# An encoder layer on one core: another order for the first weight chunks, and the modulated input with priority and in full precision on ScalarE

## The chip, the core and the metric

The kernel runs on one core of a Trainium2 chip. A core has TensorE (PE: matmuls, with weight loads shown apart as PEld), VectorE (DVE), ScalarE (ACT), GpSimd (POOL), and SyncE (SP), whose queue issues most transfers. Each engine works through its own queue in order; semaphores join them. The metric is device time in microseconds (us): the median of the runs.

## The reference

One layer of an encoder: 256 tokens of width 2048, all in float32. The part that matters here is the start: six modulation vectors from the condition c, the modulated input, and the projection to q, k and v.

```python
c_act = jax.nn.silu(c)
mod = c_act @ mod_w[i] + mod_b[i]
sh_m, sc_m, g_m, sh_f, sc_f, g_f = jnp.split(mod, 6, axis=-1)
hmix = x * (1.0 + sc_m[:, None, :]) + sh_m[:, None, :]
proj = h @ w_qkv + b_qkv        # h is hmix, (256, 2048) @ (2048, 3072)
...
x = layer_norm(DEEPNORM_ALPHA * x + (1.0 + g_m[:, None, :]) * y, ...)
hff = x * (1.0 + sc_f[:, None, :]) + sh_f[:, None, :]
u = jnp.square(jax.nn.relu(hff @ w1 + b1))
```

Behind the projection come windowed attention with rotary positions and sinks, the output projection, a layer norm, and an MLP of 8192 hidden units with a second layer norm.

## The kernel before

**Precision.** A matmul of two float32 operands is made of three matmuls in a rounded format. Each operand is split into a high part (the value rounded) and a low part (the value less its high part). The three products are high by high, high by low and low by high; low by low is left out. `mm3` (line 497) issues the three for one output of 128x512 and one 128-row tile of the inner dimension. Its three lines are 498, 499 and 500. The output gathers in a PSUM bank, a `pa` tile. There are five such banks.

**Weights.** All large weights come in chunks of 128x2048 float32 (1,024 KB) through one list, planned ahead of time. `Stream.loads` issues their transfers on SP's queue, in the order of the list, whenever one of eight buffers is free. ScalarE copies each half of a chunk to its high part (`wh`, line 247), and VectorE subtracts to get the low part (`wl`, line 218). There are five buffers for each. `Stream.pump` does this ahead of the matmuls.

**Modulation.** The list also holds chunks of the modulation weights. Such a chunk is used up at once by `Mod.step`: either PE multiplies it by c into the bank `pm` (line 307), or VectorE accumulates it into a tile (lines 343 and 345). The last chunk of a group closes the sum: four matmuls add VectorE's part, and ScalarE copies the result to `mrow` (line 361).

**Groups.** The inner dimension of 2048 has 16 tiles of 128. They are cut into six groups of 1, 1, 2, 4, 4 and 4 tiles, so that the projection can start before the whole modulation is known. Groups 0 and 1 share the first three weight chunks (`FIRST`); groups 2 to 5 have chunks of their own, 3 or 6 each. When group g's modulation is complete, `modulated(g)` makes the group's input: `columns` transposes `mrow` on PE (lines 370 and 377) and adds the bias on VectorE (371, 373 and 383, 384). Then for each tile ScalarE makes the high part of x * scale + shift (line 519), VectorE makes the same in full precision (line 520), and VectorE subtracts to get the low part (line 521).

**Projection.** `qkv_first` works on the first three chunks and `qkv` on the others. For each chunk and each of the two halves of 128 tokens a bank gathers 3 matmuls per tile. `evict` then empties the banks: the first time by a copy on ScalarE (line 535), later by an addition on VectorE (line 537). Some chunks (`CARRY`) leave their banks open for the next.

**What sets the order.** The transfers follow the list, written at lines 425 to 449. Within an engine the order is set by a scheduler when the program is built: it takes the instructions in the order of the code, moves them by its own estimates of time, and may let one overtake another. `tc.keep_in_program_order` pins an instruction; `Stream.pinned` does so while `S.pin` is set, that is, up to line 624. The code from line 604 to 633 runs the groups one after another: `S.vecs(n)` uses up n modulation chunks, `run(qkv(g, c), mid)` runs a weight chunk and calls `mid` after its first half.

Of the kernel before, what the change touches and what calls it, by code (L numbers as in the profile page):

```python
# [2 lines left out]

# [1 line left out]

# [6 lines left out]
F32 = mybir.dt.float32  # L12
F32R = mybir.dt.float32r
I32 = mybir.dt.int32
AF = mybir.ActivationFunctionType
OP = mybir.AluOpType
# [4 lines left out]
S = 256  # L21
NT = S // 128
# [26 lines left out]
def hybrid_kernel(ctx: ExitStack, tc: tile.TileContext, a, out: bass.AP):  # L49
    nc = tc.nc  # L50
    cst = ctx.enter_context(tc.tile_pool(name="cst", bufs=1))
    sml = ctx.enter_context(tc.tile_pool(name="sml", bufs=4))
# [21 lines left out]
    def g4(dt=F32):  # L74
        return gen.tile([128, 1024], dt, tag="g4", name="g4")

    def f32(x):
        return x.bitcast(F32)
# [5 lines left out]
    modmb, modfb, lnT = (pack[:, 80 + 32 * n:112 + 32 * n].rearrange("p (n k) -> p n k", n=2) for n in range(3))  # L84
# [340 lines left out]
    wq = lambda g, c: S.plan(a["wqkv"][m_mix[g][1] * 6 // 4 + c])  # L425
    m_mix[0][0].plan(2)
    S.plan(a["wqkv"][0])
    m_mix[1][0].plan(2)
    S.plan(a["wqkv"][1])
    S.plan(a["wqkv"][2])  # L430

    S.side[len(S.q)] = lambda: load_x(1)
    m_mix[2][0].plan(3)
    wq(2, 1)
    m_mix[2][0].plan(1)
    for g in range(2, G):
        n = len(ORDER[g])
        if g + 1 < G:
# [58 lines left out]
    def mm3(ps, xh, xl, wh, wl, start, stop):  # L497
        nc.tensor.matmul(ps, xh, wh, start=start, stop=False)  # L498
        nc.tensor.matmul(ps, xh, wl, start=False, stop=False)  # L499
        S.prev = nc.tensor.matmul(ps, xl, wh, start=False, stop=stop).ins  # L500
# [3 lines left out]
    def load_x(n):  # L504

        k0, nk = XK[n]
        xt = g4()
        (nc.sync if n else nc.scalar).dma_start(xt[:, :nk * 256], a["xT"][:, k0 * 256:(k0 + nk) * 256])
        for k in range(nk):
            xts[k0 + k] = xt[:, k * 256:k * 256 + 256]  # L510

    def modulated(g):
        m, k0, nk = m_mix[g]
        columns(m, modmb, (scm, shm), k0, nk)
        hh, hl = g4(F32R), g4(F32R)
        for k in range(nk):
            s = slice(k * 256, k * 256 + 256)
            xt, sc, sh = xts.pop(k0 + k), scm[:, k0 + k:k0 + k + 1], shm[:, k0 + k:k0 + k + 1]
            tc.keep_in_program_order(nc.scalar.activation(hh[:, s], xt, AF.Identity, scale=sc, bias=sh))  # L519
            tc.keep_in_program_order(nc.vector.tensor_scalar(xt, xt, sc, sh, op0=OP.mult, op1=OP.add))  # L520
            tc.keep_in_program_order(nc.vector.tensor_sub(hl[:, s], xt, f32(hh[:, s])))  # L521
        held[g] = hh, hl

    half = {}
# [17 lines left out]
    def qkv_first(n):  # L542

        wh, wl = S.main()
        for i, (g, p) in enumerate(FIRST[n]):
            hh, hl = held[g]
            c = CORD[p]
            opens = c not in half
            held_back = ((g, n), p) in CARRY or (n == 1 and g == 0)
            pss = half.pop(c, None) or banks()  # L550
            for t in range(NT):
                s = slice(t * 128, t * 128 + 128)
                mm3(pss[t], hh[:, s], hl[:, s], wh(i), wl(i), opens, c in acc and not held_back)
            if i % 2:
                S.done()
            if held_back:
                half[c] = pss
            else:
                evict(c, pss)
            if i == 1:  # L560
                yield

    def qkv(g, ch):

        _, k0, nk = m_mix[g]
        hh, hl = held[g]
        wh, wl = S.main()
        per = 4 // nk
        for ci in range(per):
            p = ch * per + ci  # L570
            c = CORD[p]
            go_on, held_back = c in half, ((g, ch), p) in CARRY
            pss = half.pop(c, None) or banks()
            for k2 in range(0, nk, 2):
                for t in range(NT):
                    for k in (k2, k2 + 1):
                        s = slice(k * 256 + t * 128, k * 256 + t * 128 + 128)
                        mm3(pss[t], hh[:, s], hl[:, s], wh(ci * nk + k), wl(ci * nk + k),
                            k == 0 and not go_on, k == nk - 1 and not held_back)
                S.done()  # L580
                if per == 1 and k2 == 0:
                    yield
            if held_back:
                half[c] = pss
            else:
                evict(c, pss)
            if per == 2 and ci == 0:
                yield

    def run(gen, mid=()):  # L590
        next(gen)
        for f in mid:
            f()
        for _ in gen:
            pass
# [16 lines left out]
    idle(6)  # L612
    msk = masks()
    S.nh, S.nl = 5, 4
    S.pace = 1
    run(qkv_first(0))
    S.vecs(2)
    run(qkv_first(1), [lambda: modulated(1)])
    trig = rotary_tables()
    run(qkv_first(2))  # L620
    S.vecs(4)
    modulated(2)
    S.pace = VECS
    S.pin = False
    for x, (g, c) in enumerate(qk_order):
# [208 lines left out]
    for n in range(21):  # L834
# [35 lines left out]
        if n == 12:  # L870
            g1 = gate(m_gm)
        if n == 16:
            warm = sml.tile([128, 1], F32, name="warm")
            nc.scalar.activation(warm, eps, AF.Sqrt)
            st = [sml.tile([128, 4, 6], F32, name=f"st{t}", bufs=2) for t in range(NT)]


# [298 lines left out]
```

## Time and profile before

| | before |
|---|---|
| median of 3 runs | 1095.94 us (1095.34 to 1098.32) |
| the profiled execution | 1100.0 us, its span 1098.2 us |
| PE idle from 0 to 75.45 us | 10.85 us |
| PE idle from 75.45 to 140 us | 2.23 us |
| PE idle from 140 to 231 us | 0.22 us |
| PE idle from 231 us to the end | 17.27 us |
| mean granted clock of PE | 0.991 |

The idle times are the length of a stretch less PE's busy time in it. In a row of the timeline the columns are start, duration (both in us), engine, line, operation, the tile written, the tiles read, shapes, and the count; in brackets stands the idle time in front and what ended it. Matmul ends are modelled and overlap: a matmul of 128x512 is shown with 0.39 us, but the next starts 0.23 us later. "x16" for a modulation step on PE is one chunk.

### The profile page before, as it was taken

How to read it: one execution, taken by the hardware profiler on the slowest of the kernel's cores; microseconds unless marked ns; L12 is line 12 of the kernel's file. 1: busy time of each engine (PE TensorE's matmuls, PEld its weight loads, DVE VectorE, ACT ScalarE, POOL GpSimd, SP SyncE). 2: the span in 40 equal slices, each digit the busy share in tenths (PEclk: the TensorE clock that was granted, in tenths of full speed). 3: DMA queues.
4: the chain of work that ended last, by engine and by line, in shares of the span. 5: the costliest groups of instructions: out<-in, count | busy, mean ns of one | idle time of the engine just before them, and what ended most of it. 6: DMA issues, size and time to landing. Idle time of an engine off the chain costs nothing.

```text
span 1098.2 us, 15487 instructions
## 1 busy us (share of the span) xinstructions
PE 1067.6 (97%) x6098; PEld 863.1 (79%) x6098; DVE 804.2 (73%) x1162; ACT 522.0 (48%) x806; POOL 30.0 (3%) x54
## 2 busy tenths in 40 slices
PE   8889999998999999999999999999999999999995
PEld 6657677665677799988888888888888888888884
DVE  4597899978899877754588889756666557665676
ACT  5333346765673537643344543344453334544340
POOL 1000000001000000000000010001000000000001
PEclk9989999999999999999999999999999999999998
DMA  9999987789985996555578788866555555557511
GB/s 384 425 427 425 427 357 280 271 297 379 377 315 201 361 360 244 185 192 192 195 301 303 272 313 306 312 220 225 184 189 190 197 196 186 178 185 267 191 75 77
DMA packets 43337, 292.70 MB, mean 267 GB/s; under 512 B 5104, under 2 KB 5232, under 8 KB 9472
## 3 DMA queue, kind: packets, MB, share of 16 engines
q1 hardware_dynamic: 39312, 279.85, 66.9%
q0 software_dynamic: 3200, 10.50, 2.7%
q10 hardware_dynamic: 752, 1.35, 0.3%
q8 instruction: 48, 0.79, 0.3%
q14 instruction: 25, 0.20, 0.0%
HBM read 289.57 MB, written 2.11 MB: 266 GB/s over the span
## 4 chain that ended last, share of the span: by engine, by line
PE 86%; DVE 7%; DMA 4%; ACT 2%; issue 1%; DVEq 0%; ACTq 0%
PE pa L995 16%; PE pa L500 15%; PE pa L498 15%; PE pa L499 15%; PE pa L996 8%; PE pa L972 3%; PE pa L971 3%; PE pa L973 3%; PE pm L307 3%; DVE wl L218 2%; DMA raw<-in_modm 2%; DMA raw<-in_modf 1%; DVE g L345 1%; DMA raw<-in_wqkv 1%; PE pa L687 1%; PE pa L743 1%
## 5 line engine op out<-in xcount | busy, mean ns | idle before, releaser
L218 DVE TENSOR_TENSOR wl<-raw,wh 128x1024 fp32r<-128x1024 f32 x332 | 403.9, 1223 | 223.6 <-ACT wh L247 222.9
L247 ACT CAST wh<-raw 128x1024 fp32r<-128x1024 f32 x332 | 347.1, 1051 | 441.3 <-PE pa L500 228.6
L498 PE MATMUL pa<-wh,g 128*128 128x512 f32 x816 | 324.1, 398 | 5.1 <-ACT g L519 2.6
L500 PE MATMUL pa<-wh,g 128*128 128x512 f32 x816 | 318.9, 392 | 4.1 <-DVE g L521 3.0
L499 PE MATMUL pa<-wl,g 128*128 128x512 f32 x816 | 320.0, 392 | 0.0
L995 PE MATMUL pa<-g,wh 128*128 128x512 f32 x768 | 270.1, 397 | 0.0
L996 PE MATMUL pa<-g,wl 128*128 128x256 f32 x768 | 214.9, 280 | 0.0
L498 PEld LDWEIGHTS pa<-wh,g 128*128 128x128 f32 x816 | 153.9, 189 | 46.8 <-issue 7.5
L500 PEld LDWEIGHTS pa<-wh,g 128*128 128x128 f32 x816 | 153.5, 188 | 41.2 <-DVE g L521 6.0
L499 PEld LDWEIGHTS pa<-wl,g 128*128 128x128 f32 x816 | 153.9, 189 | 33.0 <-issue 2.4
L995 PEld LDWEIGHTS pa<-g,wh 128*128 128x128 f32 x768 | 144.2, 188 | 36.0 <-issue 0.8
L996 PEld LDWEIGHTS pa<-g,wl 128*128 128x128 f32 x768 | 144.8, 189 | 0.1
L345 DVE SCALAR_TENSOR_TENSOR g<-raw,cact,g 128x1024 f32<-128x1024 f32 x65 | 82.6, 1280 | 2.8 <-DMA raw<-in_modf 2.3
L972 PE MATMUL pa<-g,wh 128*128 128x256 f32 x256 | 72.7, 285 | 0.4 <-DVE g L915 0.4
L971 PE MATMUL pa<-g,wh 128*128 128x256 f32 x256 | 72.5, 286 | 0.0
L973 PE MATMUL pa<-g,wl 128*128 128x256 f32 x256 | 72.3, 283 | 0.0
L307 PE MATMUL pm<-raw,cact 128*32 128x256 f32 (+2 forms) x776 | 48.8, 375 | 5.9 <-DMA raw<-in_modf 3.2
L971 PEld LDWEIGHTS pa<-g,wh 128*128 128x128 f32 x256 | 48.8, 192 | 1.3 <-issue 0.8
L972 PEld LDWEIGHTS pa<-g,wh 128*128 128x128 f32 x256 | 49.1, 192 | 0.9 <-DVE g L915 0.8
L973 PEld LDWEIGHTS pa<-g,wl 128*128 128x128 f32 x256 | 49.1, 192 | 0.0
L345 DVE SCALAR_TENSOR_TENSOR g4b<-raw,cact,g4b 128x1024 f32<-128x1024 f32 x32 | 40.7, 1280 | 9.0 <-DMA raw<-in_modgf 8.8
L307 PEld LDWEIGHTS pm<-raw,cact 128*32 128x32 f32 x776 | 20.9, 112 | 25.9 <-issue 11.5
(165 smaller groups left out, 741.6 us busy)
## 6 DMA issues: line engine op xcount, KB each, us to landing
raw<-in_w SPq DMA_DIRECT2D x64, 1024.0 KB, 4.9
raw<-in_w1b SPq DMA_DIRECT2D x48, 1024.0 KB, 5.0
raw<-in_modm SPq DMA_DIRECT2D x32, 1024.0 KB, 14.8
raw<-in_modf SPq DMA_DIRECT2D x32, 1024.0 KB, 6.9
raw<-in_wqkv SPq DMA_DIRECT2D x24, 1024.0 KB, 12.8
raw<-in_modgm SPq DMA_DIRECT2D x16, 1024.0 KB, 7.5
raw<-in_wo SPq DMA_DIRECT2D x16, 1024.0 KB, 7.5
raw<-in_w1a SPq DMA_DIRECT2D x16, 1024.0 KB, 7.6
```

What stands on the lines that cost most here:

```text
L218: self.pinned(nc.vector.tensor_sub(l, r, f32(self.hs[n])))
L247: self.pinned(nc.scalar.copy(h, s))
L307: i = nc.tensor.matmul(self.ps[32 * j:32 * j + 32, :w], lhsT[j] if type(lhsT) is list else lhsT, rhs[j], start=self.first, stop=stop)
L345: nc.vector.scalar_tensor_tensor(p[:, :e], s, cact[:, kt:kt + 1], p[:, :e], op0=OP.mult, op1=OP.add)
L498: nc.tensor.matmul(ps, xh, wh, start=start, stop=False)
L499: nc.tensor.matmul(ps, xh, wl, start=False, stop=False)
L500: S.prev = nc.tensor.matmul(ps, xl, wh, start=False, stop=stop).ins
L971: nc.tensor.matmul(o, wh(w, 128), hh, start=new, stop=False)
L972: nc.tensor.matmul(o, wh(w, 128), hl, start=False, stop=False)
L973: nc.tensor.matmul(o, wl(w, 128), hh, start=False, stop=end)
L995: nc.tensor.matmul(ps, wh(k, 128), hb, start=k == 0, stop=False)
L996: nc.tensor.matmul(ps[:, :256], wl(k, 128), hb[:, :256], start=False, stop=k == NK - 1)
```

## The change

Six edits, all in the start of the kernel up to the end of the projection.

1. In the list of transfers the second weight chunk moves ahead of group 1's two modulation chunks, and all four of group 2's modulation chunks stand together ahead of group 2's first weight chunk.
2. The work on the first three weight chunks is cut into its twelve parts (`qkv_first` yields after each), and the modulation chunks and `modulated(1)`, `modulated(2)`, `rotary_tables()` are placed between them by hand.
3. `modulated` is put under `tc.high_priority()` for groups 3 to 5; the pinned instructions in it remain pinned for groups 0 to 2 alone.
4. In `modulated`, the full-precision x * scale + shift is made by ScalarE for all groups but the first.
5. In `qkv`, the two matmuls with the input's high part come first for both halves of the tokens and both tiles; the matmuls with the input's low part follow.
6. An activation that should load a table early (`warm`) is left out. In the program before, the scheduler had placed it at the very start of ScalarE's queue.

```diff
     m_mix[0][0].plan(2)
     S.plan(a["wqkv"][0])
+    S.plan(a["wqkv"][1])
     m_mix[1][0].plan(2)
-    S.plan(a["wqkv"][1])
     S.plan(a["wqkv"][2])
-
     S.side[len(S.q)] = lambda: load_x(1)
-    m_mix[2][0].plan(3)
+    m_mix[2][0].plan(4)
+
     wq(2, 1)
-    m_mix[2][0].plan(1)
...
     def modulated(g):
         m, k0, nk = m_mix[g]
-        columns(m, modmb, (scm, shm), k0, nk)
-        hh, hl = g4(F32R), g4(F32R)
-        for k in range(nk):
-            s = slice(k * 256, k * 256 + 256)
-            xt, sc, sh = xts.pop(k0 + k), scm[:, k0 + k:k0 + k + 1], shm[:, k0 + k:k0 + k + 1]
-            tc.keep_in_program_order(nc.scalar.activation(hh[:, s], xt, AF.Identity, scale=sc, bias=sh))
-            tc.keep_in_program_order(nc.vector.tensor_scalar(xt, xt, sc, sh, op0=OP.mult, op1=OP.add))
-            tc.keep_in_program_order(nc.vector.tensor_sub(hl[:, s], xt, f32(hh[:, s])))
+
+        with nullcontext() if S.pin else tc.high_priority():
+            columns(m, modmb, (scm, shm), k0, nk)
+            hh, hl = g4(F32R), g4(F32R)
+            for k in range(nk):
+                s = slice(k * 256, k * 256 + 256)
+                xt, sc, sh = xts.pop(k0 + k), scm[:, k0 + k:k0 + k + 1], shm[:, k0 + k:k0 + k + 1]
+                S.pinned(nc.scalar.activation(hh[:, s], xt, AF.Identity, scale=sc, bias=sh))
+                if g:
+                    S.pinned(nc.scalar.activation(xt, xt, AF.Identity, scale=sc, bias=sh))
+                else:
+                    S.pinned(nc.vector.tensor_scalar(xt, xt, sc, sh, op0=OP.mult, op1=OP.add))
+                S.pinned(nc.vector.tensor_sub(hl[:, s], xt, f32(hh[:, s])))
         held[g] = hh, hl
...
-            if i % 2:
-                S.done()
             if held_back:
                 half[c] = pss
             else:
                 evict(c, pss)
-            if i == 1:
-                yield
+            if i % 2:
+                S.done()
+            yield
...
             for k2 in range(0, nk, 2):
-                for t in range(NT):
-                    for k in (k2, k2 + 1):
-                        s = slice(k * 256 + t * 128, k * 256 + t * 128 + 128)
-                        mm3(pss[t], hh[:, s], hl[:, s], wh(ci * nk + k), wl(ci * nk + k),
-                            k == 0 and not go_on, k == nk - 1 and not held_back)
+
+                for x in range(2):
+                    for t in range(NT):
+                        for k in (k2, k2 + 1):
+                            s = slice(k * 256 + t * 128, k * 256 + t * 128 + 128)
+                            w = ci * nk + k
+                            if x == 0:
+                                nc.tensor.matmul(pss[t], hh[:, s], wh(w), start=k == 0 and not go_on, stop=False)
+                                nc.tensor.matmul(pss[t], hh[:, s], wl(w), start=False, stop=False)
+                            else:
+                                S.prev = nc.tensor.matmul(pss[t], hl[:, s], wh(w), start=False,
+                                                          stop=k == nk - 1 and not held_back).ins
                 S.done()
...
-    S.pace = 1
-    run(qkv_first(0))
+
+    S.pace = 0
+    steps = (x for n in range(3) for x in qkv_first(n))
+
+    def parts(n):
+        for _ in range(n):
+            next(steps, None)
+
+    parts(2)
+    S.vecs(1)
+    parts(1)
+    S.vecs(1)
+    modulated(1)
+    parts(4)
+    S.vecs(1)
+    trig = rotary_tables()
+    parts(1)
+    S.vecs(1)
+    parts(2)
     S.vecs(2)
-    run(qkv_first(1), [lambda: modulated(1)])
-    trig = rotary_tables()
-    run(qkv_first(2))
-    S.vecs(4)
     modulated(2)
+    parts(3)
     S.pace = VECS
...
         if n == 16:
-            warm = sml.tile([128, 1], F32, name="warm")
-            nc.scalar.activation(warm, eps, AF.Sqrt)
             st = [sml.tile([128, 4, 6], F32, name=f"st{t}", bufs=2) for t in range(NT)]
```

What the built programs make of it shows at three places. Lines of the changed kernel have other numbers: 520 and 522 are the two activations and 525 the subtraction in `modulated`, 541 the eviction on VectorE, 585, 586 and 588 the three matmuls in `qkv`.

The first place is VectorE around the second of group 4's weight chunks. `wl_1086` and `wl_1156` are that chunk's low parts, `g4_1031` is the accumulator of group 5's modulation, `pa_1070` and `pa_1071` are the banks of group 4's first weight chunk, and `g4_1108`, `g4_1109` are group 4's input, high and low. Before:

```order
L343 TENSOR_SCALAR g4_1031<-raw_864,cact_110 128x1024
L345 SCALAR_TENSOR_TENSOR g4_1031<-raw_864,cact_110,g4_1031 128x1024
L345 SCALAR_TENSOR_TENSOR g4_1031<-raw_906,cact_110,g4_1031 128x1024 x2
L218 TENSOR_TENSOR wl_1086<-raw_942,wh_1062 128x1024
L218 TENSOR_TENSOR wl_1156<-raw_942,wh_1084 128x1024
L345 SCALAR_TENSOR_TENSOR g4_1031<-raw_960,cact_110,g4_1031 128x1024
L520 TENSOR_SCALAR g4_602<-g4_602,scm_112,shm_113 128x256
L345 SCALAR_TENSOR_TENSOR g4_1031<-raw_960,cact_110,g4_1031 128x1024
L521 TENSOR_TENSOR g4_1109<-g4_602,g4_1108 128x256
```

The same place in VectorE's queue in the changed program:

```order
L345 SCALAR_TENSOR_TENSOR g4_1031<-raw_864,cact_110,g4_1031 128x1024
L525 TENSOR_TENSOR g4_1109<-g4_614,g4_1108 128x256 x4
L345 SCALAR_TENSOR_TENSOR g4_1031<-raw_906,cact_110,g4_1031 128x1024
L541 TENSOR_TENSOR g4_276<-g4_276,pa_1070 128x512
L345 SCALAR_TENSOR_TENSOR g4_1031<-raw_906,cact_110,g4_1031 128x1024
L541 TENSOR_TENSOR g4_276<-g4_276,pa_1071 128x512
L218 TENSOR_TENSOR wl_1086<-raw_942,wh_1062 128x1024
L218 TENSOR_TENSOR wl_1156<-raw_942,wh_1084 128x1024
```

The input's low part has moved ahead of the accumulations, and both evictions of the first chunk's banks now stand ahead of the second chunk's low parts. At the borders between the second and third and the third and fourth of group 3's chunks both evictions likewise stand ahead of the next low part, without an accumulation between them.

The second place is ScalarE around the end of group 5's modulation. `wh_1062`, `wh_1084` are the high parts of group 4's second weight chunk, `wh_1154`, `wh_1172` those of its third and last, `mrow_1150` is group 5's modulation and `g4_1258` the high part of group 5's input. Before:

```order
L247 CAST wh_1084<-raw_942 128x1024
L519 ACTIVATE g4_1108<-g4_602,shm_113,scm_112 128x256 x4
L361 COPY mrow_1150<-pm_1020 128x256
L247 CAST wh_1154<-raw_1056 128x1024
L247 CAST wh_1172<-raw_1056 128x1024
L247 CAST wh_1188<-raw_1060 128x1024
L247 CAST wh_1210<-raw_1060 128x1024
L247 CAST wh_1226<-raw_1066 128x1024
L247 CAST wh_1248<-raw_1066 128x1024
L519 ACTIVATE g4_1258<-g4_844,shm_113,scm_112 128x256 x4
```

The same place in ScalarE's queue in the changed program:

```order
L247 CAST wh_1084<-raw_942 128x1024
L361 COPY mrow_1150<-pm_1020 128x256
L520 ACTIVATE g4_1258<-g4_844,shm_113,scm_112 128x256 x2
L522 ACTIVATE g4_844<-g4_844,shm_113,scm_112 128x256 x2
L520 ACTIVATE g4_1258<-g4_844,shm_113,scm_112 128x256 x2
L522 ACTIVATE g4_844<-g4_844,shm_113,scm_112 128x256 x2
L247 CAST wh_1154<-raw_1056 128x1024
L247 CAST wh_1172<-raw_1056 128x1024
```

Eight activations of group 5's input now stand between the copy of its modulation and the first cast of group 4's last weight chunk; before, six casts stood there and the four activations came behind them.

The third place is PE at the same end of group 5's modulation. `pm_1020` is its bank, `pt_1252` its transposes, `pa_1196` and `pa_1197` are the banks of group 4's second chunk, `pa_1234` and `pa_1235` those of its last. Before:

```order
L500 MATMUL pa_1196<-wh_1062,g4_1109 128x512
L307 MATMUL pm_1020<-raw_1034,cact_110 32x256 x8
L307 MATMUL pm_1020<-g4_1031,onesf_95 32x256 x4
L500 MATMUL pa_1197<-wh_1062,g4_1109 128x512
L498 MATMUL pa_1197<-wh_1062,g4_1108 128x512
L499 MATMUL pa_1197<-wl_1086,g4_1108 128x512
L500 MATMUL pa_1197<-wh_1062,g4_1109 128x512
L498 MATMUL pa_1196<-wh_1084,g4_1108 128x512
```

The same place in PE's queue in the changed program:

```order
L588 MATMUL pa_1196<-wh_1084,g4_1109 128x512 x2
L588 MATMUL pa_1197<-wh_1084,g4_1109 128x512 x2
L307 MATMUL pm_1020<-raw_1034,cact_110 32x256 x8
L307 MATMUL pm_1020<-g4_1031,onesf_95 32x256 x4
L377 MATMUL pt_1252<-ident_89,mrow_1150 128x128 x2
L585 MATMUL pa_1234<-wh_1154,g4_1108 128x512
L585 MATMUL pa_1235<-wh_1154,g4_1108 128x512
L586 MATMUL pa_1234<-wl_1174,g4_1108 128x512
```

Before, 16 matmuls of group 4's second chunk and two of its last stood between the closing matmuls of the modulation and the transposes; now the transposes follow at once, and the last chunk's matmuls come behind them.

More of the change, by code (lines that the diff above doesn't have):

```diff
@@ L1 @@
 import math
-from contextlib import ExitStack
+from contextlib import ExitStack, nullcontext
 import numpy as np
```

## Prediction

> **What bounds the kernel now.** I read the page first, then the waits of PE, then busy time by stretches, then the timeline of each engine from 38 to 150 us.
>
> ```profile
> span 1098.2 us, 15487 instructions
> ...
> PE 1067.6 (97%) x6098; PEld 863.1 (79%) x6098; DVE 804.2 (73%) x1162; ACT 522.0 (48%) x806; POOL 30.0 (3%) x54
> ```
>
> TensorE (PE) is busy 97% of the span, so time is lost only where PE idles or runs slowly. The stretches say where:
>
> ```profile
> 47.00:75.45 28.45, 24.83 (x155) 16.20 (x154) 27.84 (x38) 7.09 (x10) 1.91 (x2) 0.99 1.01 426
> 75.45:140.00 64.55, 62.32 (x348) 45.33 (x349) 52.14 (x68) 22.70 (x29) 0.00 (x0) 0.95 1.01 427
> 140.00:231.00 91.00, 90.78 (x466) 63.70 (x464) 89.20 (x165) 60.56 (x138) 1.23 (x2) 1.00 0.76 297
> ```
>
> The columns are length, busy PE, PEld, DVE, ACT and POOL, granted clock, DMA share, GB/s. Up to 140 us the DMA engines are full, so a chunk of 1,024 KB arrives every 2.5 us (1.049 MB by 427 GB/s) in either order. From 140 us PE is without a gap and transfers have slack. A shift of PE at 140 us therefore reaches the end of the kernel, unless a later wait absorbs it. The two largest waits that the change can reach are these:
>
> ```profile
> PE pa L500 <- DVE g L521: 3.0, 3, 2.2
> PE pa L498 <- ACT g L519: 2.6, 2, 2.4
> ```
>
> Both are waits for the modulated input: its rounded part from ScalarE (L519) and the rest from VectorE (L521).
>
> **The change part by part.** I call weight chunk c of group g (g,c); group 4 runs (4,1), (4,2), (4,0). I compare the instant at which PE starts (4,0), the last chunk before PE stays full.
>
> Part 1, the early order and the table loads, I cost at nothing. On SP's queue one weight transfer passes the two of group 1's modulation, and the fourth of group 2's passes (2,1); nothing else moves there, and POOL's queue stays as it was. Before, the start and the second and third chunk of group 3's modulation look like this:
>
> ```profile
> 11.32 0.27 ACT L361 COPY mrow<-pm 128x128 f32<-128x128 f32 x1 [3.28 <-PE pm L307]
> ...
> 44.33 0.75 DVE L343 TENSOR_SCALAR g<-raw,cact 128x1024 f32<-128x1024 f32 x1 [4.04 <-DMA raw<-in_modm]
> 48.95 1.07 PE L307 MATMUL pm<-raw,cact 128*32 128x256 f32 x16
> ```
>
> The 44.33 is a landing, so the third chunk lands at 44.33 + 2.5 = 46.8. With its second weight chunk sooner, PE ends the first three weight chunks at about 41, not just before 48.95: the last chunk of group 2's modulation lands 5.5 chunks ahead of 46.8, at 33.2, and behind it stand at most 24 matmuls (5.5) and two modulation steps (2.2). But in the new order both of group 3's PE chunks stand ahead of nearly all of group 2's matmuls, so PE waits until 46.8, and VectorE, in order, until 44.33. The gain ends in a wait for DMA. That wait of 6 us also covers what group 1's modulation loses, one transfer or 2.5 us; without it, that would show. The two table loads and the warm-up leave ScalarE's start, where it idles 3.28 us for PE anyway.
>
> Part 2, group 3 starts sooner. Before:
>
> ```profile
> 71.25 0.17 DVE L384 TENSOR_SCALAR scm<-scm 128x4 f32<-128x4 f32 x1
> ...
> 72.90 1.99 ACT L247 CAST wh<-raw 128x1024 fp32r<-128x1024 f32 x2 [5.19 <-DMA raw<-in_wqkv]
> 74.80 2.07 ACT L519 ACTIVATE g<-g,shm,scm 128x256 fp32r<-128x256 f32 x4
> ...
> 75.45 0.79 PE L498 MATMUL pa<-wh,g 128*128 128x512 f32 x1 [2.39 <-ACT g L519]
> 76.17 1.94 PE L307 MATMUL pm<-raw,cact 128*32 128x256 f32 x16
> ...
> 90.67 1.07 PE L307 MATMUL pm<-raw,cact 128*32 128x256 f32 x16
> ```
>
> The scale was ready at 71.42, but L519 stood behind two casts that waited for a landing. Now it stands ahead. VectorE's queue from 44.33 to the scale holds 7 accumulations at 1.2, 8 low parts at 1.15, 10 evictions at 0.6 and 1.1 of others: 25.1 us, hence 69.4; PE's own work, with a stretch at half clock after its wait, gives 70.4. With 0.6 for L520, PE starts at 71.05 instead of 75.45: **-4.4**. The half clock goes too: the same step took 1.94 at 76.17 and 1.07 at 90.67, and the clock columns
>
> ```profile
> 70.00:80.00 10.00, 7.61 (x47) 3.97 (x46) 9.25 (x18) 3.97 (x6) 0.95 (x1) 0.75 1.02 429
> 80.00:90.00 10.00, 10.00 (x42) 8.19 (x41) 7.99 (x9) 4.10 (x4) 0.00 (x0) 0.91 1.01 428
> ```
>
> lost 2.5 + 0.9 = 3.4 us of clock, some of it before PE started; I take **-2.9**. The wait for L521 goes as well, since its full-precision operand now comes from ScalarE:
>
> ```profile
> 123.31 0.50 PE L500 MATMUL pa<-wh,g 128*128 128x512 f32 x1 [2.23 <-DVE g L521]
> ...
> 134.26 0.62 PE L498 MATMUL pa<-wh,g 128*128 128x512 f32 x2
> ...
> 142.32 0.50 PE L500 MATMUL pa<-wh,g 128*128 128x512 f32 x1 [0.21 <-DVE g L521]
> ```
>
> That is **-2.2**, and -0.2 at 142.32. Row 134.26 is the start of (4,0) before. From 75.45 that is 58.8 us, of which 58.8 - 2.9 - 2.2 = 53.7 is work that stays.
>
> Part 3, new waits at chunk borders. Prices, from VectorE's and PE's timeline:
>
> ```profile
> 96.71 1.28 DVE L345 SCALAR_TENSOR_TENSOR g<-raw,cact,g 128x1024 f32<-128x1024 f32 x1
> 97.90 0.68 DVE L537 TENSOR_TENSOR g<-g,pa 128x512 f32<-128x512 f32 x1
> 98.50 2.35 DVE L218 TENSOR_TENSOR wl<-raw,wh 128x1024 fp32r<-128x1024 f32 x2
> ...
> 92.00 0.40 PE L499 MATMUL pa<-wl,g 128*128 128x512 f32 x1
> 92.24 0.40 PE L500 MATMUL pa<-wh,g 128*128 128x512 f32 x1
> ```
>
> By the distances of starts an accumulation holds VectorE 1.19, an eviction 0.60, a low part 1.2; a matmul step is 0.23 and ends 0.16 behind its step. The new order does all products with the high part first, so a chunk's two banks close in its last four matmuls, and VectorE has the two evictions ahead of the next chunk's low part. PE has only 4 x 0.23 = 0.92 to cover it: two matmuls of the other bank and two that need no low part. At two borders of group 3 the wait is 0.16 + 0.60 + 0.60 + 1.2 - 0.92 = 1.65; at a third one eviction stands ahead: 1.05. At (4,1) to (4,2) an accumulation stands between the evictions: 0.16 + 0.60 + 1.19 + 0.60 + 1.2 - 0.92 = 2.85. At the end of group 5's modulation eviction, accumulation, eviction, accumulation stand ahead of PE's closing matmuls, with two matmuls and one modulation chunk as cover: 0.16 + 0.60 + 1.19 + 0.60 + 1.28 - 0.46 - 1.09 = 2.3. Together **+9.5**: the closing matmuls end at 71.05 + 53.7 + 9.5 = 134.25.
>
> Part 4, (4,0) behind group 5's modulation. Before and after it is a question of what ScalarE does next:
>
> ```profile
> 130.63 0.37 ACT L361 COPY mrow<-pm 128x256 f32<-128x256 f32 x1 [13.38 <-PE pm L307]
> 130.90 4.84 ACT L247 CAST wh<-raw 128x1024 fp32r<-128x1024 f32 x5
> ...
> 134.72 0.39 PE L377 MATMUL pt<-ident,mrow 128*128 128x128 f32 x2
> ```
>
> Before, the casts of (4,0) followed the copy at once, and PE still had 16 matmuls of (4,2). Now PE has ended (4,2), and eight activations with priority stand ahead of the cast: copy 0.4, transposes 0.45, scale 0.45, eight activations 8 x 0.52 = 4.15 (four took 2.07 above), cast 1.05: **+6.5** from 134.25 to 140.75. The full-precision activation has no row. Its ends are 0.41, VectorE's operation that it replaces, and 0.60, a whole L519 without overlap:
>
> ```profile
> 50.91 0.41 DVE L520 TENSOR_SCALAR g<-g,scm,shm 128x256 f32<-128x256 f32 x1
> ...
> 37.49 0.60 ACT L519 ACTIVATE g<-g,shm,scm 128x256 fp32r<-128x256 f32 x1
> ```
>
> L519 on the same engine and shape is nearest, so 0.52; the ends give 0.4 us less or more. Behind the first two matmuls the low part is missing for 1.2 - 0.46 = 0.75, while the transposes (0.35) no longer come there: **+0.4**. After an idle 6 us a half clock is likely, as it came after 2.39 us above. Its shorter form stands here:
>
> ```profile
> 30.00:40.00 10.00, 8.73 (x84) 6.34 (x85) 3.18 (x7) 2.85 (x4) 0.00 (x0) 0.83 1.01 424
> ```
>
> 0.17 of 10 us is **+1.7**. Bounds: nothing, and three such (behind the 2.85, the 2.3 and the 6), 5.1.
>
> The Trainium skill ("TensorE: Matmul & The Clock Gate", section on HAM oscillation) asks for idle gaps over about 3.4 us before the clock halves; the gap of 2.39 us in front of 75.45 had already brought it, so the trace does not agree with that bound. By the page only the 6 us gap pays and the sum stands; by the trace the 2.85 gap may pay too, 1.7 more.
>
> Sum: (4,0) starts at 140.75 instead of 134.26, +6.5; with 0.4, 1.7 and -0.2, **+8.4 us**. The profiled execution took 1100.0 (its span 1098.2), so 1108.4 there; it lies 4.1 above the median of 1095.94, so I put the median at **1104**. VectorE's relief of 15 operations at 0.41 (6.2 us) I cost at nothing: from 75 us it waits for PE's banks.
>
> **The rivals.** (a) Faster. The intended reading: low parts are ready at the borders, because VectorE reaches the evictions before PE needs the next chunk. Then -4.4 - 2.9 - 2.4 remain, but (4,0) itself caps it:
>
> ```profile
> L202 SPq DMA_DIRECT2D raw<-in_wqkv x1: 328/328/328, 117.9 to 117.9; - x1
> ...
> DMA to landing us min/median/max: 7.5/7.5/7.5
> ```
>
> It lands at 125.4, castable at 126.5, so at most 134.3 - 126.5 = 7.8 us: 1088. Against it: the evictions stand ahead in the queue, and ScalarE cannot cast before the activations. It decides at the (4,1) border: less than 0.5 us of wait there means this rival. (b) The change does not do what it says: the delay is absorbed. VectorE is busy 89.2 of 91 us from 140 to 231; its 6.2 us less could come back there: 8.4 - 6.2, 1098. Against it: those operations lie before 140. (c) Slower still. Six later chunks have the same matmul order with VectorE full; if each eviction is 4 x 0.23 late, 5.5 us more: 1110.
>
> **How the numbers follow.** Forecast 0.64, (a) 0.14, (b) 0.12, (c) 0.10. Forecast: 8.4 with the clock between 0 and 5.1 instead of 1.7 and the activations 0.4 either way gives 6.3 to 12.2, and my 71.05 may be off by 1.5: 1100.7 to 1109.6. The range takes in (b) and half of (c): 1094 to 1110, leaving out about 0.19. A measurement here can tell 0.3%, 3.3 us, from no change. Faster by more: (a) 0.14; within: most of (b), 0.11; slower: 0.75.
>
> **What would show it.** In the new trace: PE idle from about 41 to 47; group 3 from about 71 at full clock; no wait for L521's successor; waits of PE for low parts (L218) of 1 to 3 us between 80 and 125; one of about 6 us for a cast near 134 to 141. If PE starts (4,0) before 134, I am wrong in sign, and the border waits are where.

## The result, and the profile after

| | before | after |
|---|---|---|
| median | 1096.62 us of 4 runs (1095.34 to 1098.32) | 1109.82 us of 4 runs (1107.93 to 1111.45) |
| ratio after / before | | 1.0119, 95% interval 1.0096 to 1.0142 |
| the profiled execution | 1100.0, span 1098.2 | 1111.45, span 1109.6 |

The change makes the kernel slower: by 13.2 us in the medians, by 11.45 between the two profiled executions. The forecast was 8.4 between profiled executions and 1104 us for the median.

First the waits of PE in the changed kernel (what it waited for: us in all, times, the longest):

```profile
span 1109.6 us, 15476 instructions
...
PE pa L586 <- DVE wl L218: 7.0, 4, 2.8
PE pa L585 <- ACT wh L247: 5.5, 1, 5.5
PE pm L307 <- DMA raw<-in_modm: 4.9, 2, 3.8
...
PE pm L307 <- DVE g L345: 2.3, 1, 2.3
```

The waits for the modulated input (2.6 and 3.0 us before) are gone. In their place stand four waits for low parts at the borders between chunks, one for a cast, and one for an accumulation, ahead of the closing matmuls of group 5's modulation (the closing wait): 14.8 us together. The timeline of PE shows the three largest, and VectorE's shows what stood ahead of the low part:

```profile
122.01 0.61 PE L585 MATMUL pa<-wh,g 128*128 128x512 f32 x2
125.42 0.50 PE L586 MATMUL pa<-wl,g 128*128 128x512 f32 x1 [2.80 <-DVE wl L218]
125.76 0.48 PE L585 MATMUL pa<-wh,g 128*128 128x512 f32 x1
...
136.85 0.64 PE L307 MATMUL pm<-g,onesf 128*32 128x256 f32 x8 [2.31 <-DVE g L345]
137.99 0.44 PE L377 MATMUL pt<-ident,mrow 128*128 128x128 f32 x2 [0.49 <-ACT mrow L361]
143.91 1.22 PE L585 MATMUL pa<-wh,g 128*128 128x512 f32 x2 [5.49 <-ACT wh L247]
```

```profile
121.75 0.69 DVE L541 TENSOR_TENSOR g<-g,pa 128x512 f32<-128x512 f32 x1 [5.29 <-PE pa L588]
122.36 1.28 DVE L345 SCALAR_TENSOR_TENSOR g<-raw,cact,g 128x1024 f32<-128x1024 f32 x1
123.55 0.68 DVE L541 TENSOR_TENSOR g<-g,pa 128x512 f32<-128x512 f32 x1
124.15 2.36 DVE L218 TENSOR_TENSOR wl<-raw,wh 128x1024 fp32r<-128x1024 f32 x2
```

VectorE had been idle for 5.29 us, because the eviction at the head of its queue waited for PE to close the bank. The low part that PE needed next stood three places behind. ScalarE's timeline shows the same in front of (4,0), the chunk whose start the prediction compares: eight activations stand between the copy and the casts.

```profile
137.56 0.37 ACT L361 COPY mrow<-pm 128x256 f32<-128x256 f32 x1 [20.89 <-PE pm L307]
138.86 1.09 ACT L520 ACTIVATE g<-g,shm,scm 128x256 fp32r<-128x256 f32 x2 [0.93 <-DVE scm L384]
139.86 1.08 ACT L522 ACTIVATE g<-g,shm,scm 128x256 f32<-128x256 f32 x2
...
142.82 3.87 ACT L247 CAST wh<-raw 128x1024 fp32r<-128x1024 f32 x4
```

Last the stretches of 10 us (columns as in the prediction; the clock is the number before the last two):

```profile
120.00:130.00 10.00, 7.20 (x25) 5.47 (x24) 7.24 (x7) 0.00 (x0) 0.00 (x0) 0.83 1.02 424
130.00:140.00 10.00, 5.62 (x53) 2.67 (x51) 4.05 (x7) 1.51 (x4) 0.00 (x0) 0.98 0.74 287
140.00:150.00 10.00, 6.05 (x14) 4.33 (x15) 7.47 (x9) 7.82 (x12) 0.00 (x0) 0.51 0.89 342
```

Besides the waits PE ran at half clock. The longest such stretch lies around and behind the wait of 5.49 us, from 139.59 to 149.83.

The start of a chunk on PE is the time of its first matmul, counted at 24 matmuls a chunk (where two chunks interleave it is off by a few matmuls). These starts say where each kernel gains and loses; the experiments below stand in the same table (us):

| kernel | (3,5), start of group 3 | (4,1) | (4,0) | (5,0) | from there to PE's end |
|---|---|---|---|---|---|
| before | 75.45 | 117.80 | 134.26 | 140.09 | 945.7 |
| after | 71.61 | 115.27 | 143.91 | 152.46 | 944.7 |
| early_order_alone | 76.28 | 118.51 | 134.95 | 140.79 | 943.5 |
| matmul_order_alone | 75.37 | 115.86 | 131.58 | 137.26 | 941.9 |
| priority_alone | 73.87 | 117.41 | 138.63 | 145.12 | 946.0 |
| low_parts_ahead | 72.11 | 110.42 | 132.53 | 140.52 | 943.0 |
| casts_ahead | 71.66 | 115.37 | 139.03 | 146.69 | 943.7 |
| low_and_casts_ahead | 72.42 | 110.95 | 128.83 | 136.81 | 944.0 |

All of the loss is made before (5,0): 12.4 us, of which 1.0 comes back later.

### The profile page after: what moved, and what is told of

Its sections match the earlier page's. It is cut to its first block, busy times and chain, and to the rows that moved or that the text cites. A ratio compares the mean times of both kernels' runs of the same rounds, so it can differ in the third digit from the quotient of the medians.

```text
span 1109.6 us, 15476 instructions
## 1 busy us (share of the span) xinstructions
PE 1069.3 (96%) x6098; PEld 863.6 (78%) x6098; DVE 799.7 (72%) x1147; ACT 528.0 (48%) x818; POOL 30.0 (3%) x54
## 3 DMA queue, kind: packets, MB, share of 16 engines
HBM read 289.57 MB, written 2.11 MB: 263 GB/s over the span
## 4 chain that ended last, share of the span: by engine, by line
PE 88%; DVE 6%; DMA 3%; ACT 2%; issue 1%; DVEq 0%; ACTq 0%
PE pa L1017 16%; PE pa L497 13%; PE pa L498 13%; PE pa L499 13%; PE pa L1018 8%; PE pa L586 3%; PE pm L307 3%; PE pa L585 3%; PE pa L588 3%; PE pa L994 3%; PE pa L993 3%; PE pa L995 3%; DVE wl L218 2%; DMA raw<-in_modf 1%; DMA raw<-in_modm 1%; PE pa L711 1%
## 5 line engine op out<-in xcount | busy, mean ns | idle before, releaser
L218 DVE TENSOR_TENSOR wl<-raw,wh 128x1024 fp32r<-128x1024 f32 x332 | 403.6, 1224 | 212.6 <-ACT wh L247 211.5
L497 PE MATMUL pa<-wh,g 128*128 128x512 f32 x648 | 255.0, 395 | 0.4 <-ACT wh L247 0.4
L499 PE MATMUL pa<-wh,g 128*128 128x512 f32 x648 | 252.6, 390 | 0.0
L497 PEld LDWEIGHTS pa<-wh,g 128*128 128x128 f32 x648 | 121.7, 188 | 30.4 <-issue 2.8
L498 PEld LDWEIGHTS pa<-wl,g 128*128 128x128 f32 x648 | 121.9, 188 | 26.1 <-issue 1.0
L499 PEld LDWEIGHTS pa<-wh,g 128*128 128x128 f32 x648 | 121.8, 188 | 25.5 <-DVE g L770 0.2
L585 PE MATMUL pa<-wh,g 128*128 128x512 f32 x168 | 68.2, 416 | 5.6 <-ACT wh L247 5.5
```

Of the source, the lines that this page charges most:

```text
L218: self.pinned(nc.vector.tensor_sub(l, r, f32(self.hs[n])))
L585: nc.tensor.matmul(pss[t], hh[:, s], wh(w), start=k == 0 and not go_on, stop=False)
```

## The experiments

The kernel before ran beside each set; its median lay between 1096.4 and 1097.0 us.

| kernel | median us | ratio to before, 95% interval |
|---|---|---|
| early_order_alone | 1098.87 | 1.0021 (1.0009 to 1.0034) |
| matmul_order_alone | 1094.66 | 0.9987 (0.9969 to 1.0005) |
| priority_alone | 1105.08 | 1.0071 (1.0047 to 1.0094) |
| undo_matmul_order | 1103.66 | 1.0063 (1.0038 to 1.0087) |
| fixed_place_on_scalar | 1099.68 | 1.0017 (0.9997 to 1.0038) |
| full_precision_on_vector | 1103.12 | 1.0052 (1.0030 to 1.0073) |
| low_parts_ahead | 1097.75 | 1.0010 (0.9995 to 1.0025) |
| casts_ahead | 1105.67 | 1.0085 (1.0052 to 1.0117) |
| low_and_casts_ahead | 1093.20 | 0.9972 (0.9959 to 0.9985) |
| low_ahead_old_matmuls | 1094.00 | 0.9970 (0.9950 to 0.9991) |
| fill_the_gap | 1110.24 | 1.0125 (1.0099 to 1.0151) |
| both_ahead_and_fill | 1095.05 | 0.9973 (0.9953 to 0.9994) |

### Which edit makes the border waits

There are two theories: M, the new matmul order, as the prediction argued; and Q, VectorE's queue, which the scheduler fills otherwise once the modulated input has priority. The first kernel takes the matmul order out of the change, the second has nothing but it (edit 5 of the diff, in `qkv`).

```diff
-                for x in range(2):
-                    for t in range(NT):
-                        for k in (k2, k2 + 1):
...
+                for t in range(NT):
+                    for k in (k2, k2 + 1):
+                        s = slice(k * 256 + t * 128, k * 256 + t * 128 + 128)
+                        mm3(pss[t], hh[:, s], hl[:, s], wh(ci * nk + k), wl(ci * nk + k),
```

> The changed kernel with the matmuls of the group chunks in the order of before (per bank: high x high, high x low, low x high). Theory M (what the prediction's part 3 says: the border waits come from the new matmul order, which closes both banks in the last four matmuls): the waits of 1.6, 1.6, 1.0 and 2.8 us for low parts (L218) go, 7.0 us, and with them the 5.5 us wait for the cast and its half clock: about 1094 or below. Theory Q (they come from VectorE's queue, where the evictions stand ahead of the next low part since the modulated input has priority and no fixed place; the order of the instructions still shows two evictions ahead of the low parts of the third, fourth and fifth chunk of group 3 and of the second of group 4): by 0.16 + 0.60 + 1.20 - 0.46 a wait of 1.5 us stays at each of three borders of group 3 and one of about 1.9 at (4,1) to (4,2), 6.4 together; the 5.5 us wait for the cast goes, since two more casts now stand ahead of group 5's eight activations: 1098, between 1095 and 1101.

> The kernel before with the new matmul order and nothing else of the change. ScalarE's queue stays as before, and on VectorE every low part of groups 3 to 5 still has two or three evictions of the chunk ahead of it behind it. Theory M: four border waits of 1.0 to 2.8 us and the closing wait of 2.3 come, 9.3 us: about 1106. Theory Q: no wait for a low part above 0.5 us, the waits of 2.4 and 2.2 us for the modulated input stay: 1096.6, within 2.

Without the new matmul order the waits stay; with it alone none comes. First the waits of undo_matmul_order, then of matmul_order_alone:

```profile
PE pa L498 <- DVE wl L218: 7.3, 6, 1.9
PE pm L307 <- DMA raw<-in_modm: 5.7, 2, 3.8
PE pm L307 <- DMA raw<-in_modf: 2.9, 2, 1.8
PE pm L307 <- DVE g L345: 2.3, 1, 2.3
```

```profile
PE pa L581 <- ACT g L519: 3.0, 2, 2.0
PE pm L307 <- DMA raw<-in_modm: 2.8, 3, 1.4
...
PE pa L584 <- DVE g L521: 2.0, 3, 1.2
```

In the first the waits at the four borders measured 1.46, 1.45, 1.46 and 1.90 us, as worked out for Q (1.5, 1.5, 1.5, 1.9). Its time was not: the median lies 7.2 above that of before (1103.66 to 1096.49), where 1.4 was expected, and above the range of Q (1095 to 1101). The closing wait of 2.3 stayed too, which that number had left out. Between the spans it is only 3.2 (1101.4 to 1098.2), because before's profiled execution lies 3.5 above before's median. The second has no low part (L218) in its list at all. M falls and Q stands: 1094.66 is no measurable difference from before.

The next two divide the rest: the modulated input alone as the change has it, and the early order alone.

> The kernel before with only the modulated input changed (priority, no fixed place, full precision on ScalarE); early order and matmul order as before. All theories: group 3 starts about 71 at full clock instead of 75.45, and the waits for L519 and L521 go, -9.7 us with the half clock. Theory M: nothing else, 1087. Theory Q: three border waits of 1.5 in group 3 and one of 1.9 in group 4 take 6.4 back, and the closing matmuls of group 5's modulation may wait up to 2.3: between 1093 and 1096. Theory E (the early order causes the loss): 1087 too.

> Only the early order of the first weight chunks (and the two table loads that leave); modulated input and matmul order as before. The prediction's part 1 (nothing): PE ends the first three weight chunks near 41, waits for landings until about 47.5, and group 3 starts between 75.0 and 76.0 as before; 1096.6 within 2. Theory E (the early order costs, through the idle 41 to 47 and a half clock behind it): group 3 starts 2 us or more later and the time is 1100 or above.

The waits of priority_alone for low parts:

```profile
PE pa L499 <- DVE wl L218: 6.8, 5, 1.9
```

The modulated input alone costs 8.6 us, two thirds of the loss. The four border waits come (6.3 of these 6.8 us), the closing 2.3 too, and group 3 starts at 73.87, 2.9 later than expected (1.2 of it a wait for a bank). The time came out 9 us above the range of Q. The later start and a half clock behind the last border, 1.7, are half of that. Another 3.3 is no mechanism: I added to the traces' times, where it lies 5.3 above before, and not 8.6 as in the medians. The early order alone (with edit 6, which goes along in that kernel) starts group 3 0.8 us later and costs 2.5 us, 0.3 above the range expected: little, but more than nothing.

Priority and ScalarE's longer list are two edits. One kernel takes the priority away and pins the instructions to their place again, the other brings the full precision back to VectorE:

```diff
-        with nullcontext() if S.pin else tc.high_priority():
...
-                S.pinned(nc.scalar.activation(hh[:, s], xt, AF.Identity, scale=sc, bias=sh))
...
+            tc.keep_in_program_order(nc.scalar.activation(hh[:, s], xt, AF.Identity, scale=sc, bias=sh))
```

```diff
-                if g:
+                if False:
```

> The changed kernel without the priority: the modulated input stands in a fixed place of the program again, its full-precision part still on ScalarE. VectorE's order of evictions and low parts is that of before (every low part of groups 3 to 5 but (4,1)'s ahead of the evictions). If the priority made the loss: no border waits, no wait of 5.5, but group 3 starts about 76.2 again (early order alone: 76.28) with up to 1.5 more for the longer row of activations: 1098.5, between 1096.5 and 1101. Rival, if the move to ScalarE made it: 1105 or above.

> The changed kernel with the full-precision part back on VectorE, with priority as in the change. Evictions stand ahead of low parts at the same borders as in the change, so the waits of 1.6, 1.6, 1.0 and about 2.5 stay, and perhaps the closing 2.3; four activations instead of eight and two more casts ahead of them take the 5.5 away, with its half clock (2.9); four operations of 0.41 more on VectorE in front of each group's input, up to 2.2: 1102.5, between 1100 and 1105. Rival, if the move to ScalarE made the loss: 1096.

One line of the waits of each, of fixed_place_on_scalar and then of full_precision_on_vector:

```profile
PE pa L582 <- ACT g L519: 4.7, 3, 3.9
```

```profile
PE pa L586 <- DVE wl L218: 7.3, 5, 2.8
```

Both came out as expected. With a fixed place no border wait is left (1099.68); there PE waits for the modulated input again. With priority but VectorE's arithmetic the border waits are 1.61, 1.59, 1.01 and 2.81 us (1103.12). Edit 3 does two things, however: it gives priority and it takes the pin away. No run has one without the other, so which of the two moves the evictions is not shown; "priority" below means both. Over all these kernels the waits go with one thing, the number of evictions that stand in VectorE's queue ahead of the next chunk's low parts:

| kernel | evictions ahead at (3,3), (3,0), (3,2), (4,2) | waits there, us |
|---|---|---|
| before, early_order_alone, matmul_order_alone, fixed_place_on_scalar | 0, 0, 0, 0 | none for a low part |
| after, full_precision_on_vector | 2, 2, 1, 2 | 1.61, 1.58, 1.01, 2.80 (after) |
| priority_alone, undo_matmul_order | 2, 2, 2, 2 | 1.46, 1.45, 1.46, 1.89 (priority_alone) |

### Mending the queues

If the queue is the cause, putting the low parts ahead must remove the waits and leave everything else of the change. An order-only dependency does that:

```diff
-                nc.vector.tensor_add(av, av, pss[t])
+                i = nc.vector.tensor_add(av, av, pss[t])
+                n = 2 * S.im + 1
+                if S.hot and n < len(S.lows):
+                    tc.add_manual_dep(i.ins, S.lows[n], ORDER_ONLY, reason="behind")
```

`S.lows` lists the low parts, `S.im` counts the chunks begun, and `S.hot` is set in groups 3 to 5.

> The changed kernel, with one thing more: in groups 3 to 5 each eviction on VectorE has to stand behind both low parts of the next chunk (order on the engine only). ScalarE's queue is unchanged. If the border waits are evictions standing ahead of low parts, the waits of 1.6, 1.6, 1.0 and 2.8 us go (7.0 us) and the half clock behind the 2.8 (1.7): about 1101; the wait of 5.5 us for (4,0)'s cast and its half clock stay. Rival (VectorE is simply full there): PE waits as long for a bank as it did for a low part, and the time stays at 1110.

The waits of PE in that kernel (its lines are numbered up to 6 higher), and VectorE at the border of (4,1) to (4,2):

```profile
PE pa L591 <- ACT wh L250: 5.5, 1, 5.5
PE pm L310 <- DMA raw<-in_modm: 5.1, 3, 3.9
PE pm L310 <- DMA raw<-in_modf: 2.9, 2, 1.8
```

```profile
115.79 2.36 DVE L219 TENSOR_TENSOR wl<-raw,wh 128x1024 fp32r<-128x1024 f32 x2 [0.93 <-ACT wh L250]
118.07 1.28 DVE L348 SCALAR_TENSOR_TENSOR g<-raw,cact,g 128x1024 f32<-128x1024 f32 x1
119.26 0.68 DVE L544 TENSOR_TENSOR g<-g,pa 128x512 f32<-128x512 f32 x1
```

The low parts are made before the evictions and no border wait is left. VectorE is not full there: in the changed kernel it idled 5.29 us with the eviction at the head of its queue. The time falls by 12.1 us, not by 8.7: the closing wait of 2.3 goes too, since the accumulations behind come earlier. The 5.5 us stays. The next kernel mends that one alone (`S.casts` lists the casts), and the one behind it both:

```diff
-                S.pinned(nc.scalar.activation(hh[:, s], xt, AF.Identity, scale=sc, bias=sh))
+                i = nc.scalar.activation(hh[:, s], xt, AF.Identity, scale=sc, bias=sh)
+                S.pinned(i)
+                if g == G - 1:
+                    tc.add_manual_dep(i.ins, S.casts[2 * S.im - 1], ORDER_ONLY, reason="behind")
```

> The changed kernel with one thing more: on ScalarE the first activation of group 5's modulated input has to stand behind both casts of (4,0). VectorE's evictions keep their places, so the border waits of 1.6, 1.6, 1.0, 2.8 and 2.3 stay. If the 5.5 us wait is the eight activations in front of the cast, it goes (with the 0.9 us of the transposes' copy about 6.4), and with it the half clock over (4,0), 2.9 us; about 1 us of waits comes at (5,0), as without the new matmul order: about 1101.5, between 1099 and 1104. Rival (the cast waits for its chunk's landing or its buffer): the wait stays above 3 us and the time above 1106.

> Both orders mended in the changed kernel: evictions of groups 3 to 5 behind the next chunk's low parts, group 5's activations behind (4,0)'s casts. low_parts_ahead took 1097.75; the 5.5 us wait and the half clock over (4,0) (2.3 us in that run) go, about 1 us comes at (5,0): 1091, between 1089 and 1094, ahead of both kernels. Rival: VectorE or the landings take the gain back, 1096.

ScalarE in casts_ahead:

```profile
137.65 0.37 ACT L364 COPY mrow<-pm 128x256 f32<-128x256 f32 x1 [20.95 <-PE pm L310]
137.92 2.00 ACT L248 CAST wh<-raw 128x1024 fp32r<-128x1024 f32 x2
139.82 1.09 ACT L523 ACTIVATE g<-g,shm,scm 128x256 fp32r<-128x256 f32 x2
```

(4,0) starts at 139.03 instead of 143.91. The casts run at once behind the copy, and PE's wait for them is 0.51 us: the wait of 5.5 us was the activations. The median fell by 4.2 us (by 6.8 between the traces), less than the 8.3 expected, to 1.7 above the range: a half clock of 3.41 us stayed over (4,0). Both together beat the kernel before by 0.28%, within the range expected. The last of this set keeps the matmul order of before:

> The changed kernel with evictions behind low parts in groups 3 to 5 and the matmul order of before (two casts of (4,0) then stand ahead of group 5's activations by themselves). From undo_matmul_order (1103.66) the border waits of 7.3 and the closing wait of 2.3 go: 1094, between 1092 and 1096.5, the same as low_and_casts_ahead (1093.2). If the matmul order is worth something by itself, 1096 or above.

It took 1094.00 us against 1093.20: the matmul order is worth nothing that shows.

### The half clock

Is the half clock behind the 5.5 us a cost of its own? `fill(22)` puts 22 matmuls on constants on PE behind group 5's transposes; nothing else changes.

```diff
+        if g == G - 1:
+            fill(22)
         held[g] = hh, hl
```

> The changed kernel with 22 matmuls on constants (128x512, 0.23 us each, 5.0 us) on PE in the 5.5 us in front of (4,0). The wait itself stays in place, so (4,0) starts at about 143.9 as in the changed kernel. If the gap alone costs, the time stays at 1110. If a half clock behind it costs besides, (4,0) to (5,0) takes 5.7 us instead of 8.5 at full clock and the time is about 1107.

PE in that kernel, and its clock:

```profile
138.33 5.26 PE L613 MATMUL pt<-onesr 128*128 128x512 f32 x22
144.08 0.73 PE L587 MATMUL pa<-wh,g 128*128 128x512 f32 x2 [0.49 <-ACT wh L247]
```

```profile
130.00:140.00 10.00, 7.20 (x60) 4.20 (x60) 4.04 (x7) 1.35 (x3) 0.00 (x0) 1.00 0.78 292
140.00:150.00 10.00, 8.99 (x38) 6.79 (x37) 7.64 (x10) 8.89 (x13) 0.00 (x0) 1.00 0.87 341
```

(4,0) starts where it did (144.08), the clock is 1.00 instead of 0.51, and (4,0) to (5,0) takes 6.38 us instead of 8.55. So the half clock cost 2.2 us there. At the end of PE's work 1.0 is left of it, and the median (1110.24, where 1107 was expected) shows nothing of it: the runs span 1107.05 to 1111.6.

The same filling in the kernel with both queues mended:

> low_and_casts_ahead with 5 matmuls on constants (1.15 us) in the wait of 1.18 us in front of (4,0). In the traces so far every stretch of 3.41 us of the clock's own grid in which PE idled 1.77 us or more was followed by half clock, and of those under 1.74 none. The window ahead of (4,0) had 1.98 us idle there and a half clock of 3.41 us behind it; with the fill it has at most 1.1, so no half clock comes between 125 and 140 in any execution, and (4,0) to (5,0) takes about 6.3 us instead of 7.98: 1091.5, within 1.5. If the rule is wrong, the half clock stays and the time is 1093.2.

Between 120 and 140 us its clock is 1.00, and (4,0) to (5,0) took 6.38 us instead of 7.98, as expected. The median did not follow: 1095.05, where 1091.5 within 1.5 was expected. In its profiled execution two other waits further on, for DMA (2.11 and 2.31 us), were each followed by a half clock:

```profile
260.00:270.00 10.00, 10.00 (x54) 7.27 (x52) 8.21 (x16) 5.24 (x15) 2.87 (x4) 0.92 1.01 416
...
360.00:370.00 10.00, 9.42 (x63) 5.96 (x64) 4.51 (x16) 6.91 (x13) 0.00 (x0) 0.83 0.99 411
```

What happens in the other executions no trace shows; all ten scatter from 1090.45 to 1098.41. The two longest (1098.22 and the profiled one) have the lowest mean granted clock, 0.990; the others have 0.991 to 0.994.

## Why the prediction was right, and where it was not

**Sign and waits: right.** Group 3 started sooner (at 71.61; the forecast was 71.05), the waits at chunk borders and the closing wait took it back (9.31 us; forecast 9.5), and eight activations ahead of the cast did the rest (6.42 from the closing matmuls' end to (4,0); forecast 6.5). Which edit causes the border waits the prediction had wrong (part 3).

**Part 1: nearly.** PE ended the first three chunks at 41.46 and then waited until 47.47, but for one step: the gain ends in a wait for DMA. Alone the early order cost 2.5 us, and group 3 started 0.8 us later. Beside the modulated input's edits it cost nothing that shows: undo_matmul_order has it and priority_alone has not, group 3 starts at 72.76 and 73.87, and the medians are 1103.66 and 1105.08.

**Part 2: right between the traces.** No wait for the low part of the modulated input is left, and the half clock behind the start of group 3 is gone. But that half clock (2.9 of the gain) need not come in every execution of the kernel before: matmul_order_alone waited 2.00 us at the same place and ran at full clock from 70 to 90 us. By the part's own prices VectorE's queue adds up to 24.7 us and not 25.1; nothing hangs on it, since the later 70.4 of PE was used.

**Part 3: numbers right, reason wrong.** The prediction said: "The new order does all products with the high part first, so a chunk's two banks close in its last four matmuls, and VectorE has the two evictions ahead of the next chunk's low part." The first half is not the cause of the second. The matmul order alone leaves every low part ahead of the evictions, as it was; the priority fills the queue otherwise, with either matmul order. The matmul order only moves a wait from 1.45 to 1.6, from 1.9 to 2.8 where an accumulation stands between, and from 1.46 to 1.0 where it leaves one eviction ahead. Two edits that were priced together, at places read in the final queues, hid which one had written them.

**Part 4: right for the wait.** That it needs three edits together (priority, ScalarE's longer list and the matmul order) was not seen. Without any one of them (fixed_place_on_scalar, full_precision_on_vector, undo_matmul_order) both casts of (4,0) stand ahead of the activations, and no wait for a cast there is longer than 0.5 us.

**The mis-sized term: the half clock.** I put one, 1.7 us, with 5.1 as its bound. Two came between the start of group 3 and (5,0). Behind the 2.80 us wait it covers a full 3.41 us of work, hence 1.7; over (4,0) it cost 2.2 by the filling. That is 3.9, 2.2 more than in the sum. With 0.6 for the later start of group 3 and 1.2 spread over the stretch to the closing matmuls, 2.2 + 0.6 + 1.2 makes up about the 4.0 by which (5,0) is later than 8.4. Of the 1.2 some 0.4 is the first matmul behind each of the four border waits (0.34 to the next start, as from 125.42 to 125.76, instead of 0.23); the rest I can't name. One microsecond came back behind (5,0).

**From the sum to the median.** I took 4.1 off, as before's profiled execution lay above its median. After's lies only 1.6 above. That offset belonged to one execution and not to the kernel. It makes 2.5 of the 5.8 us by which the median (1109.82) misses 1104; the trace (1111.45) is 3.1 from its own forecast (1108.4). The mean granted clock of an execution goes with its time: over the 69 executions of before that ran beside the experiments the median is 1100.5 us for the 11 with a mean clock of 0.991 or less, and 1095.4 for the 26 with 0.995 or more; the profiled one had 0.991. That the median lies within 1094 to 1110 at all is partly luck: it is 0.2 above the forecast's own stretch (1100.7 to 1109.6), and the range was drawn to 1110 to take in half of rival (c).

**The rivals.** (a) The border at (4,1) decides by its own mark, 0.5 us: it was 2.80. (b) The delay is not absorbed: 12.4 us at (5,0), 11.4 at the end. (c) Its 1110 is the number that came nearest, but its mechanism did not come: from (5,0) on the changed kernel is 1.0 us shorter, not longer.

## What to carry to other kernels

Priority for one operation (here with its pin taken away) can change more than its own place: the scheduler filled the queues around it otherwise. So read where the operations that others wait for now stand, on each engine, and price that queue rather than the edit that was meant. An engine that works in order and idles at the head of its queue, with work behind that another engine waits for, is the sign; an order-only dependency at that place gave back 12.1 us here. Try the edits apart before one of them is blamed, and compare medians with medians: one profiled execution lay 3.5 us off the median of its own kernel.

## What the hardware showed unexpectedly

The half clock came in stretches of one, two or three times 3.41 us, and within an execution up to the end of PE's work all of them began on one grid of 3.41 us. In the traces of all 14 kernels I added up PE's idle time in each such window from 20 to 1080 us, while the clock was full:

| idle in a window of 3.41 us | the next window |
|---|---|
| 1.77 us or more | half clock 28 times, full twice (1.78 and 1.83 us) |
| up to 1.74 us | full every time |

So in these traces a window counts, not a gap, and the bound lies near half of it; PE's ends are modelled, so it is known to about 0.1 us at best. The expectation for both_ahead_and_fill had said "every" of the windows from 1.77 us up, which the two exceptions contradict. Three gaps in one window (0.77, 0.49 and 0.51 in casts_ahead, 1.77 together) were enough; a gap of 2.23 us that two windows shared (before, at 123.31) was not. Where a gap falls on the grid differs between executions: the first full clock, which lies on the grid, came at 4.92 to 7.69 us in the 14 traces. Two kernels had the same wait at the same border, priority_alone 1.89 us and undo_matmul_order 1.90; their rows from 120 to 130 us, in that order:

```profile
120.00:130.00 10.00, 8.11 (x35) 5.97 (x28) 7.00 (x7) 1.04 (x1) 0.00 (x0) 0.86 0.83 323
```

```profile
120.00:130.00 10.00, 8.10 (x38) 6.24 (x35) 7.23 (x7) 1.05 (x1) 0.00 (x0) 1.00 1.00 415
```

In the first the gap fell into one window, in the second 0.15 us of it lay outside, with 1.74 us inside. The Trainium skill ("TensorE: Matmul & The Clock Gate", section "What's actually happening") says that the window is free-running and 3413 ns long; the traces agree. The Trainium skill ("TensorE: Matmul & The Clock Gate", section "HAM oscillation") asks for idle gaps over about 3.4 us; by these windows about half of that is enough. A window at half clock was followed by full clock when PE idled up to 0.18 us in it, and once 0.50; with 0.47, and with 0.77 or more, it was not. What decides there is open.
